# Twelve early column tiles instead of seven in the prologue of an adaLN and RWKV-7 kernel

## The chip, the cores and the metric

The kernel runs on one core of a Trainium2 chip. The metric is the device time of one execution in microseconds; the time of before is the median of three executions. A separate, profiled execution gives the trace: every instruction's start and end on TensorE (PE, its weight loads PEld), VectorE (DVE), ScalarE (ACT), GpSimd (POOL) and the queue SyncE (SP), which issues the DMA transfers. "L82" is line 82 of the kernel before.

## What is computed

One layer of a hybrid sequence model, for 128 context tokens and 256 latent tokens (T = 384 columns in all), with D = 2048 and 32 heads of 64. Cut to what matters:

```
mod = silu(c) @ ada_w + ada_b            # shift, scale, gate; for c and c_ctx
h   = rmsnorm(x, g) * (1 + scale) + shift
z   = h @ w_in                           # all projections, one wide matrix
r, k, v, wd, ad = token_shift(z[:N_SHIFTED])
g_a, b_gate, c_gate, x_b, g_b, m_a, m_b = split(z[N_SHIFTED:])
decay, a = f(tanh(wd) @ w2), sigmoid(a0 + ad @ a2)      # low rank, two directions
y   = bidirectional RWKV-7 scan(S0, r, decay, k, v, kk, a), group-normed, plus bonus
y_a = (y * silu(g_a)) @ w_out_a
y_b = (b_gate * conv3(c_gate * x_b) * silu(g_b)) @ w_out_b
out = x + gate * ((sigmoid(m_a) * y_a + sigmoid(m_b) * y_b) @ w_o)
```

The results are the normed outputs of both token groups and the scan's final context states.

## The kernel before

Everything is held transposed: 128 channels on the partitions, 384 tokens along the row. All large weights are float32 and are split into a high part (a cast by ACT) and a low part (a subtraction by DVE; `split`, L85). One product of a 128x128 weight block with 384 tokens is then three matmuls (`mm3`, L80): high by high, high by low, low by high. Such a triple is called a unit below, and 16 units, one for each block of 128 rows of D, make one column tile.

**Prologue (L370 to L389).** The modulation needs all of `ada_w`, and h only comes piece by piece: in round g of eight, PE multiplies four pieces of `ada_w` (tiles `raw_adah`, 128x4x512, PSUM tile `pada`), `make_h` turns row blocks 2g and 2g+1 of x into h (`h_hi`, `h_lo`), and from then on units on those two row blocks may run. Seven column tiles of `w_in` (three with the low-rank wd and ad, r of head-pair block 0, k of 0, v of 0 and 1) are accumulated meanwhile, each in a PSUM bank of its own over all eight rounds (`pe`). `early_load` fetches their rows for a round as one tile `eraw` and splits it; `pops(n)` takes n units from a list between the steps. All these loads stand in one queue on SP, in program order.

**Stream (`Stream`, L111).** The other column tiles come in pairs, 32 units a pair, through the tiles `raw`, `whi`, `wlo`: `rk{b}` (r and k of block b), `gv{b}` (the gate of block b and v of block b+1), and fillings for the convolution branch and the merge gates (`bc`, `bx`, `bg`, `gb`, `ma`, `mb`). `ds_.go(n)` issues the next n units; `ds_.until(tag)` goes on until a pair is done.

**Blocks (L937 on).** For each of 16 head-pair blocks b: `prep_b` builds the operands `pr` and `bk` of the chunk products, matmul `pA` starts the block, `prep_c` and a chain of small DVE operations (`U`, `ut`) with DMA in between invert the chunk matrices, then `scan` runs: matmul `pH` with its copies into `x`, `po`, `pbn`, `pX` with its copies into `A`, `pq`, and the rest. `scan` yields 3, 3 and 4 stream units after pH, po and pX (H0, H0, H1). Between the inversion and the scan stand a loop that streams until `gv{b}` is done, then `prep_a(b + 1)` (low-rank products `pl`, decay, the key norm `pn`, `kn`, and the scan `L`), then what is left of a window of 80 units. `norm` and, one block later, `finish` close a block.

**What sets the order.** PE executes the order in which the program is written (`manual_schedule`). The rows of DVE, ACT, POOL and SP are put in order by a scheduler, which places an instruction by the time at which it thinks it can start and by priority; on the chip each engine then runs its own list in that order. Buffers come from pools with a number of slots for each tag, and a new tile waits until the last user of its slot is done.

Of the kernel before, what the change touches and what calls it, by code (L numbers as in the profile page):

```python
# [56 lines left out]
def hybrid_step(ctx, tc, cst, x_prompt, x_sample, state_f, state_b, c, c_ctx, ada_w, ada_b, norm_g,  # L57
# [36 lines left out]
    PRO, WINDOW, FIRST, LAST = 32, 80, 24, 16  # L94
# [115 lines left out]
    ecols = ((O_WD, 3 * P), (O_R, P), (O_K, P), (O_V, 2 * P))  # L210
    NE = 7
    EW = NE * P
    banks = []
    for i in range(NE):
        pe = (pd if i < 3 else pps).tile([P, 512], F32, tag="d" if i < 3 else f"e{i}", name=f"pe_{i}")
        banks.append(pe)
    epss = [pe[:, 0:T] for pe in banks]

    xt = []
    for i, tg in enumerate(("ehi1", "elo1", "elo0")):  # L220
        xi = pp.tile([P, D], F32, tag=tg, name=f"xt{i}")
# [49 lines left out]
    def ada_load(rp, nm, cols, i, rbufs):  # L271
        raw = rp.tile([P, 4, 512], F32, tag="araw", name=f"raw_ada{nm}_{i}", bufs=rbufs)
# [870 lines left out]
```

## Time and profile before

| | before |
|---|---|
| median of 3 executions | 2264.56 us (2261.35 to 2266.23) |
| profiled execution | 2259.46 us, of which the span 2257.7 us |
| mean granted clock of PE | 0.996 |
| DVE, ACT, POOL busy | 1522.4, 1048.9, 118.6 us |
| DMA | 339.97 MB, mean 151 GB/s |

The span is the time from the first to the last instruction that the trace holds; the execution's own time is a little longer. A row of a timeline reads: start, duration, engine, line, operation, output <- inputs, shapes, number of equal instructions in a row, and in brackets the engine's idle time before it with what ended it. In a view of groups the mean duration in ns stands behind the sum.

### The profile page before, as it was taken

The page shows a single profiled execution, that of the slowest core. Times are in us where ns is not written, and L with a number is a line of the kernel's source. Part 1 is how long each engine was busy: PE and PEld are TensorE (multiplying, and loading weights), DVE is VectorE, ACT ScalarE, POOL GpSimd, SP SyncE. Part 2 cuts the span into 40 slices and gives each one's busy share as a digit, 9 for nine tenths or more (in the row PEclk, how much of TensorE's full clock was granted, in tenths as well). Part 3 has the DMA queues.
Part 4 walks back from the last instruction along what each step waited for, and adds up shares of the span by engine and source line. Part 5 has one row for each costly group of instructions (what it writes and reads, how often), then busy time and mean ns, then how long its engine had stood idle before and what let it go on. Part 6 is the DMA issues. An engine that isn't in the chain of part 4 may idle for free.

```text
span 2257.7 us, 40435 instructions
## 1 busy us (share of the span) xinstructions
PE 2187.7 (97%) x16084; PEld 2072.2 (92%) x16084; DVE 1522.4 (67%) x3096; ACT 1048.9 (46%) x1852; POOL 118.6 (5%) x115
## 2 busy tenths in 40 slices
PE   5999999999999999999999999999999999999998
PEld 3588999999999999999999999999999899889988
DVE  3249567777777778776878687777767774444444
ACT  4246445454545455454545454545455543333233
POOL 2001010101010100000010101010100000000000
PEclk9999999999999999999999999999999999999999
DMA  9963544444444444353444444444445465985633
GB/s 334 347 203 116 147 137 126 114 121 114 110 132 112 125 116 126 105 132 102 122 108 132 111 112 127 113 115 141 121 118 143 133 187 161 309 299 190 219 131 113
DMA packets 429646, 339.97 MB, mean 151 GB/s; under 512 B 84801, under 2 KB 411025, under 8 KB 428561
## 3 DMA queue, kind: packets, MB, share of 16 engines
q1 hardware_dynamic: 427968, 335.62, 50.6%
q8 instruction: 127, 2.08, 0.4%
q10 hardware_dynamic: 432, 1.57, 0.2%
q14 instruction: 63, 0.51, 0.1%
q0 software_dynamic: 1056, 0.19, 0.1%
HBM read 307.37 MB, written 29.36 MB: 149 GB/s over the span
## 4 chain that ended last, share of the span: by engine, by line
PE 90%; DMA 5%; DVE 2%; issue 2%; SPq 1%; ACT 1%; POOLq 0%; POOL 0%; DVEq 0%; ACTq 0%
PE d_rk L81 4%; PE d_gv L81 4%; PE d_gv L83 4%; PE d_gv L82 4%; PE d_rk L83 4%; PE d_rk L82 4%; DMA raw_adah<-in_ada_w_dram 3%; PE d_oa L81 2%; PE d_bx L81 2%; PE d_bg L81 2%; PE d_bc L81 2%; PE d_mb L81 2%; PE pq L822 2%; PE d_bg L83 2%; PE d_bg L82 2%; PE d_bx L83 2%
## 5 line engine op out<-in xcount | busy, mean ns | idle before, releaser
L716 DVE TENSOR_TENSOR ut<-U 48x30 f32<-48x30 f32 (+14 forms) x480 | 154.6, 322 | 16.2 <-DMA U<-ui 4.2
L81 PE MATMUL d_rk<-h_hi,whi_rk 128*128 128x384 f32 x480 | 164.3, 342 | 0.6 <-ACT lst L549 0.6
L718 DVE TENSOR_TENSOR U<-U,ut 48x30 f32<-48x30 f32 (+14 forms) x480 | 154.3, 321 | 10.8
L81 PE MATMUL d_gv<-h_hi,whi_gv 128*128 128x384 f32 x480 | 161.1, 336 | 0.0
L83 PE MATMUL d_gv<-h_hi,wlo_gv 128*128 128x384 f32 x480 | 160.8, 335 | 0.0
L82 PE MATMUL d_gv<-h_lo,whi_gv 128*128 128x384 f32 x480 | 160.7, 335 | 0.0
L83 PE MATMUL d_rk<-h_hi,wlo_rk 128*128 128x384 f32 x480 | 160.5, 334 | 0.0
L82 PE MATMUL d_rk<-h_lo,whi_rk 128*128 128x384 f32 x480 | 160.5, 334 | 0.0
L88 ACT CAST whi_gv<-raw_gv 128x1024 fp32r<-128x1024 f32 (+1 forms) x64 | 64.0, 999 | 141.1 <-PE d_rk L82 93.9
L89 DVE TENSOR_TENSOR wlo_rk<-raw_rk,whi_rk 128x1024 fp32r<-128x1024 f32 x60 | 72.9, 1218 | 44.6 <-ACT whi_rk L88 35.5
L88 ACT CAST whi_rk<-raw_rk 128x1024 fp32r<-128x1024 f32 x60 | 63.0, 1053 | 78.7 <-PE d_bx L82 16.4
L910 POOL TENSOR_TENSOR rs<-var,nhalf 128x6 f32<-128x6 f32 x16 | 21.2, 1326 | 1370.2 <-DVE var L908 1370.2
L81 PE MATMUL d_bg<-h_hi,whi_bg 128*128 128x384 f32 x256 | 92.8, 363 | 0.0
L81 PE MATMUL d_gb<-h_hi,whi_gb 128*128 128x384 f32 x256 | 92.5, 361 | 0.0
L81 PE MATMUL d_bc<-h_hi,whi_bc 128*128 128x384 f32 x256 | 92.4, 361 | 0.0
L81 PE MATMUL d_bx<-h_hi,whi_bx 128*128 128x384 f32 x256 | 92.3, 361 | 0.0
L81 PE MATMUL d_ma<-h_hi,whi_ma 128*128 128x384 f32 x256 | 92.0, 359 | 0.0
L81 PEld LDWEIGHTS d_rk<-h_hi,whi_rk 128*128 128x128 f32 x480 | 90.1, 188 | 1.8 <-ACT lst L549 0.9
L81 PEld LDWEIGHTS d_gv<-h_hi,whi_gv 128*128 128x128 f32 x480 | 90.5, 189 | 0.2
L81 PE MATMUL d_mb<-h_hi,whi_mb 128*128 128x384 f32 x256 | 90.6, 354 | 0.0
L82 PEld LDWEIGHTS d_gv<-h_lo,whi_gv 128*128 128x128 f32 x480 | 90.4, 188 | 0.0
L83 PEld LDWEIGHTS d_gv<-h_hi,wlo_gv 128*128 128x128 f32 x480 | 90.4, 188 | 0.0
(320 smaller groups left out, 6649.5 us busy)
## 6 DMA issues: line engine op xcount, KB each, us to landing
raw_adah<-in_ada_w_dram SPq DMA_DIRECT2D x64, 512.0 KB, 8.7
raw_rk<-in_w_in_dram SPq DMA_DIRECT2D x60, 512.0 KB, 5.3
raw_gv<-in_w_in_dram SPq DMA_DIRECT2D x60, 512.0 KB, 5.0
raw_ma<-in_w_in_dram SPq DMA_DIRECT2D x16, 1024.0 KB, 5.5
raw_mb<-in_w_in_dram SPq DMA_DIRECT2D x16, 1024.0 KB, 5.4
raw_bc<-in_w_in_dram SPq DMA_DIRECT2D x16, 1024.0 KB, 5.6
raw_bx<-in_w_in_dram SPq DMA_DIRECT2D x16, 1024.0 KB, 5.5
raw_bg<-in_w_in_dram SPq DMA_DIRECT2D x16, 1024.0 KB, 5.4
```

The source lines that it names most:

```text
L81: TE.matmul(out, wh, xh, start=start, stop=False)
L82: TE.matmul(out, wh, xl, start=False, stop=False)
L83: TE.matmul(out, wl, xh, start=False, stop=stop)
L88: S.copy(hi[0:rows], src)
L89: V.tensor_tensor(lo[0:rows], src, hi[0:rows].bitcast(F32), ALU.subtract)
L716: V.tensor_tensor(tv, U[:, 0:s, s:s + 1].broadcast_to([48, s, w]), U[:, s:s + 1, s + 1:].broadcast_to([48, s, w]), ALU.mult)
L718: V.tensor_tensor(U[:, 0:s, s + 1:], U[:, 0:s, s + 1:], tv, ALU.add)
L822: TE.matmul(pq[:, d, :], A[:, 0, f, :], sav[:, f, :], start=True, stop=True)
L910: G.tensor_tensor(rs[:], var[:], nhalf[:], ALU.pow)
```

## The change

The prologue now computes twelve column tiles: the seven of before, and the gate of block 0, r and k of block 1, and the two tiles of `ma0`. Five of them (wd/ad and ma0) keep a PSUM bank over all rounds. The other seven are summed in SBUF (`eacc`): in each round the two row blocks of a tile go into one of two rotating banks `er` with six matmuls, and then ACT copies (round 0) or DVE adds (rounds 1 to 7, 49 times) the bank to the sum. The early columns of a round come as three pieces of 128x2x512 through a ring of three; the norm's scratch tile uses the same ring; the pieces of `ada_w` use three buffers of their own and the two of the stream's `raw`. The units taken between the steps go from 14 to 24 a round. `rk1`, the gate of block 0 and `ma0`, 80 units, leave the stream. r, k, v and the gate move to a pool that is opened ahead of the prologue. `prep_a(b + 1)` moves behind the filling of the window, which becomes 79 units (93 in block 0, where it was 104), less the 12 that prep_a streams itself; it waits for `rk{b+1}` instead of `gv{b}`, and `finish(b - 1)` waits for `gv{b - 1}`.

```diff
-    PRO, WINDOW, FIRST, LAST = 32, 80, 24, 16
+    PRO, WINDOW, FIRST, LAST, PA = 32, 79, 14, 16, 12
...
-    ecols = ((O_WD, 3 * P), (O_R, P), (O_K, P), (O_V, 2 * P))
-    NE = 7
-    EW = NE * P
-    banks = []
-    for i in range(NE):
-        pe = (pd if i < 3 else pps).tile([P, 512], F32, tag="d" if i < 3 else f"e{i}", name=f"pe_{i}")
-        banks.append(pe)
-    epss = [pe[:, 0:T] for pe in banks]
+    ecols = (((O_WD, 3 * P), (O_GA, P)), ((O_R, 2 * P), (O_K, 2 * P)), ((O_V, 2 * P), (O_MA, 2 * P)))
+    banks, eacc = {}, {}
+    for i in (0, 1, 2, 10, 11):
+        banks[i] = (pd if i < 3 else pps).tile([P, 512], F32, tag="d" if i < 3 else f"e{i}", name=f"pe_{i}")
+    for i, (nm, b) in enumerate((("ga", 0), ("r", 0), ("r", 1), ("k", 0), ("k", 1), ("v", 0), ("v", 1))):
+        eacc[3 + i] = kp.tile([P, T], F32, tag=nm, name=f"{nm}_{b}")
+    epss = {i: banks[i][:, 0:T] for i in banks}
...
-        junk = pp.tile([P, 512], F32, tag="junk", name=f"junk_{s}")
+        junk = pp.tile([P, 2, 512], F32, tag="eraw", name=f"junk_{s}", bufs=3)
...
     def early_load(g):
-        raw = wp.tile([P, 2, EW], F32, tag="raw", name=f"eraw_{g}", bufs=2)
-        o = 0
-        for c0, w in ecols:
-            nc.sync.dma_start(raw[:, :, o:o + w], win[:, 2 * g:2 * g + 2, c0:c0 + w])
-            o += w
-        return split(raw[:], [P, 2, EW], f"ehi{g % 2}", f"elo{g % 2}", pp, f"{g}")
-
-    def early_mm(k, hl, i):
-        sl = slice(i * P, (i + 1) * P)
-        mm3(epss[i], hl[0][:, k % 2, sl], hl[1][:, k % 2, sl], h_hi[k], h_lo[k], k == 0, k == KC - 1)
+        res = []
+        for j, piece in enumerate(ecols):
+            raw = pp.tile([P, 2, 512], F32, tag="eraw", name=f"eraw_{g}_{j}", bufs=3)
+            o = 0
+            for c0, w in piece:
+                nc.sync.dma_start(raw[:, :, o:o + w], win[:, 2 * g:2 * g + 2, c0:c0 + w])
+                o += w
+            if g % 2 == 0:
+                res.append(split(raw[:], [P, 2, 512], "whi", "wlo", wp, f"e{g}_{j}"))
+            else:
+                hl = pp.tile([P, 2, 2, 512], F32R, tag=f"eo{j}", name=f"ehl_{g}_{j}")
+                S.copy(hl[:, 0], raw[:])
+                V.tensor_tensor(hl[:, 1], raw[:], hl[:, 0].bitcast(F32), ALU.subtract)
+                res.append((hl[:, 0], hl[:, 1]))
+        return res
+
+    def early_mm(g, e, hl, i):
+
+        hi, lo = hl[i // 4]
+        sl = slice(i % 4 * P, (i % 4 + 1) * P)
+        k = 2 * g + e
+        if i in epss:
+            mm3(epss[i], hi[:, e, sl], lo[:, e, sl], h_hi[k], h_lo[k], k == 0, k == KC - 1)
+            return
+        if e == 0:
+            banks["er"] = pps.tile([P, 512], F32, tag="er", name=f"er_{g}_{i}", bufs=2)
+        ps = banks["er"][:, 0:T]
+        mm3(ps, hi[:, e, sl], lo[:, e, sl], h_hi[k], h_lo[k], e == 0, e == 1)
+        if e == 1:
+            if g == 0:
+                S.copy(eacc[i][:], ps)
+            else:
+                V.tensor_tensor(eacc[i][:], eacc[i][:], ps, ALU.add)
...
+    def araw_load(g, ac, j):
+        if (4 * g + j) % 5 < 2:
+            return ada_load(wp, f"h{g}", ac, j, 2, "raw")
+        return ada_load(pp, f"h{g}", ac, j, 3)
...
-            pops(2 if g == 1 else (3, 4, 3, 2)[j])
+            pops(3 if g == 1 else (5, 6, 5, 4)[j])
         make_h(g, m5, pa)
-        pops(2)
-        queue += [(2 * g + e, hl, i) for e in range(2) for i in range(NE)]
+        pops(4)
+        keep, pas = [0, 1, 2, 10, 11], list(range(3, 10))
+        queue += [(g, 0, hl, i) for i in keep]
+        for n, i in enumerate(pas):
+            queue += [(g, 0, hl, i), (g, 1, hl, i)] + [(g, 1, hl, i2) for i2 in keep[n:n + 1]]
...
-    ds_.fills = fills
-    add_rk(1)
-    ds_.add("gv0", win, (O_GA,), hx, lambda i, ps: take_gate(0, ps))
+    ds_.fills = fills[1:]
+    ds_.done.add("gv0")
...
+    for i in range(2):
+        take_m(ma_d, "ma")(0, i, epss[10 + i])
     ctx_pro.close()
...
         if prev is not None:
+            ds_.until(f"gv{b - 1}")
             finish(b - 1, prev)
...
         if b < NB - 1:
-            while f"gv{b}" not in ds_.done:
+            while b > 0 and f"rk{b + 1}" not in ds_.done:
                 ds_.go(1)
                 n += 1
-            n += drive(prep_a(b + 1, nxt))
         w = WINDOW + (FIRST if b == 0 else LAST if b == NB - 1 else 0)
+        if b < NB - 1:
+            w -= PA
         if n < w:
             ds_.go(w - n)
+        if b < NB - 1:
+            drive(prep_a(b + 1, nxt))
```

PE in the prologue before, behind the first piece of `ada_w` in round 6 (`pada` is the modulation, `pe` an early tile, numbered by bank; `ehi` and `elo` are the parts of the seven columns of round 4):

```order
L289 MATMUL pada_784<-raw_adah_0_787,condw_pro 32x512 x4
L81 MATMUL pe_98<-h_hi_78,ehi_4_615 128x384
L82 MATMUL pe_98<-h_lo_82,ehi_4_615 128x384
L83 MATMUL pe_98<-h_hi_78,elo_4_616 128x384
L81 MATMUL pe_99<-h_hi_78,ehi_4_615 128x384
L82 MATMUL pe_99<-h_lo_82,ehi_4_615 128x384
L83 MATMUL pe_99<-h_hi_78,elo_4_616 128x384
L81 MATMUL pe_100<-h_hi_78,ehi_4_615 128x384
L82 MATMUL pe_100<-h_lo_82,ehi_4_615 128x384
L83 MATMUL pe_100<-h_hi_78,elo_4_616 128x384
L289 MATMUL pada_784<-raw_adah_1_803,condw_pro 32x512 x4
```

After, at the same place, from the second unit behind that piece on (`er` is a rotating bank, `whi_e_1` and `whi_e_2` are the second and the third of the three pieces):

```order
L81 MATMUL er_7_1076<-h_hi_78,whi_e_1_799 128x384
L82 MATMUL er_7_1076<-h_lo_82,whi_e_1_799 128x384
L83 MATMUL er_7_1076<-h_hi_78,wlo_e_1_800 128x384
L81 MATMUL er_7_1076<-h_hi_78,whi_e_1_799 128x384
L82 MATMUL er_7_1076<-h_lo_82,whi_e_1_799 128x384
L83 MATMUL er_7_1076<-h_hi_78,wlo_e_1_800 128x384
L81 MATMUL pe_102<-h_hi_78,whi_e_2_806 128x384
L82 MATMUL pe_102<-h_lo_82,whi_e_2_806 128x384
L83 MATMUL pe_102<-h_hi_78,wlo_e_2_807 128x384
L81 MATMUL er_8_1087<-h_hi_78,whi_e_2_806 128x384
L82 MATMUL er_8_1087<-h_lo_82,whi_e_2_806 128x384
L83 MATMUL er_8_1087<-h_hi_78,wlo_e_2_807 128x384
```

Before, each unit goes to a bank of its own, three of them between two pieces of `ada_w`; after, two units in a row fill a rotating bank (six matmuls), a unit on a fixed bank (`pe_102`) follows, and five units stand between the pieces.

DVE beside the scan of block 7, while block 8 is prepared, before: from the first row on the key norm on (`kn`, `kd`, `sig`, `L`, `bk` belong to block 8; `x`, `sav`, `bon`, `A` to block 7):

```order
L636 TENSOR_SCALAR kn_10260<-pn_10257 128x384
L651 TENSOR_SCALAR kd_0_10270<-sig_2_10237,par,omka 128x384
L638 RECIPROCAL kn_10260<-kn_10260 128x128 x2
L849 COPY x_7_9794<-pH_10283 32x6x32
L638 RECIPROCAL kn_10260<-kn_10260 128x128
L849 COPY x_7_9794<-pH_10283 32x6x32
L639 SCALAR_TENSOR_TENSOR kn_10260<-kk_10165,kn_10260 128x384
L806 TENSOR_TENSOR sav_9805<-po_1_0_10321,sav_9805 64x2x128
L652 TENSOR_TENSOR kd_0_10270<-k_10027,kd_0_10270 128x384
L653 TENSOR_TENSOR sig_2_10237<-kn_10260,sig_2_10237 128x384
L646 SCALAR_TENSOR_TENSOR L_1_10274<-cs,sig_1_10213 128x384
L859 TENSOR_TENSOR bon_10352<-pbn_10349,v_9017 128x384
```

and right behind them:

```order
L89 TENSOR_TENSOR wlo_bg_0_0_10336<-raw_bg_0_10333,whi_bg_0_0_10335 128x1024
L863 COPY A_9632<-pX_10354 32x6x32
L651 TENSOR_SCALAR kd_1_10278<-sig_3_10249,par,omka 128x384
L667 TENSOR_TENSOR bk_0_10712<-sig_2_10237,sig_0_10201 128x6x64
L863 COPY A_9632<-pX_10354 32x6x32
```

After, from the same first row on:

```order
L680 TENSOR_SCALAR kn_10566<-pn_10563 128x384
L695 TENSOR_SCALAR kd_0_10576<-sig_2_10543,par,omka 128x384
L682 RECIPROCAL kn_10566<-kn_10566 128x128 x3
L696 TENSOR_TENSOR kd_0_10576<-k_10296,kd_0_10576 128x384
L683 SCALAR_TENSOR_TENSOR kn_10566<-kk_10473,kn_10566 128x384
L690 SCALAR_TENSOR_TENSOR L_1_10580<-cs,sig_1_10509 128x384
L697 TENSOR_TENSOR sig_2_10543<-kn_10566,sig_2_10543 128x384
L712 TENSOR_TENSOR bk_0_11004<-kd_0_10576,sig_0_10497 128x6x64
L711 TENSOR_TENSOR bk_0_11004<-sig_2_10543,sig_0_10497 128x6x64
L695 TENSOR_SCALAR kd_1_10584<-sig_3_10555,par,omka 128x384
L89 TENSOR_TENSOR lwl_0_11618<-lraw_0_11615,lwh_0_11617 96x256
L696 TENSOR_TENSOR kd_1_10584<-k_10296,kd_1_10584 128x384
```

and right behind them:

```order
L697 TENSOR_TENSOR sig_3_10555<-kn_10566,sig_3_10555 128x384
L712 TENSOR_TENSOR bk_1_11010<-kd_1_10584,sig_1_10509 128x6x64
L711 TENSOR_TENSOR bk_1_11010<-sig_3_10555,sig_1_10509 128x6x64
L819 TENSOR_TENSOR kd_0_10576<-kd_0_10576,kd_1_10584 128x384
L820 SCALAR_TENSOR_TENSOR kd_0_10576<-kd_0_10576,par,r_10276 128x384
L893 COPY x_7_10113<-pH_10589 32x6x32 x2
L850 TENSOR_TENSOR sav_10124<-po_1_0_10627,sav_10124 64x2x128
L89 TENSOR_TENSOR wlo_gb_0_1_10533<-raw_gb_0_10526,whi_gb_0_1_10532 128x1024
L903 TENSOR_TENSOR bon_10648<-pbn_10645,v_9274 128x384
L907 COPY A_9935<-pX_10650 32x6x32
```

Before, the copies into x (L849) stand among the reciprocals, and the first copy into A (L863) ahead of all of `bk`. After, the rows for `bn` (L697), `bk` (L711, L712) and the bonus sum (L819, L820) of block 8 stand ahead of the copies into x (L893) and into A (L907).

More of the change, by code (lines that the diff above doesn't have):

```diff
@@ L199, in hybrid_step @@
     cT = cp.tile([P, 32], F32, tag="cT", name="cT")
+    ctx_kp = ExitStack()
+    kp = ctx_kp.enter_context(tc.tile_pool(name="kp", bufs=2))
     ctx_pro = ExitStack()
@@ L207, in hybrid_step @@
     nc.sync.dma_start(crow[16:32], c[0].rearrange("(k p) -> k p", p=P))
-    ecols = ((O_WD, 3 * P), (O_R, P), (O_K, P), (O_V, 2 * P))
-    NE = 7
-    EW = NE * P
-    banks = []
-    for i in range(NE):
-        pe = (pd if i < 3 else pps).tile([P, 512], F32, tag="d" if i < 3 else f"e{i}", name=f"pe_{i}")
-        banks.append(pe)
-    epss = [pe[:, 0:T] for pe in banks]
+    ecols = (((O_WD, 3 * P), (O_GA, P)), ((O_R, 2 * P), (O_K, 2 * P)), ((O_V, 2 * P), (O_MA, 2 * P)))
[5 more added lines that the diff above has]
+    epss = {i: banks[i][:, 0:T] for i in banks}
     xt = []
-    for i, tg in enumerate(("ehi1", "elo1", "elo0")):
-        xi = pp.tile([P, D], F32, tag=tg, name=f"xt{i}")
+    for i in range(3):
+        xi = pp.tile([P, D], F32, tag=f"eo{i}", name=f"xt{i}")
         nc.sync.dma_start(xi[:], x_prompt[0] if i == 0 else x_sample[0, (i - 1) * P:i * P])
@@ L269, in cond_weights, with ada_load @@
         return cw
-    def ada_load(rp, nm, cols, i, rbufs):
-        raw = rp.tile([P, 4, 512], F32, tag="araw", name=f"raw_ada{nm}_{i}", bufs=rbufs)
+    def ada_load(rp, nm, cols, i, rbufs, tag="araw"):
+        raw = rp.tile([P, 4, 512], F32, tag=tag, name=f"raw_ada{nm}_{i}", bufs=rbufs)
         o = 0
@@ L316, in x_norm @@
     def x_norm(s):
-        junk = pp.tile([P, 512], F32, tag="junk", name=f"junk_{s}")
+        junk = pp.tile([P, 2, 512], F32, tag="eraw", name=f"junk_{s}", bufs=3)
         for q in range(4):
-            S.activation(junk[:], xt[s][:, 512 * q:512 * q + 512], AF.Square, accum_out=ss4[:, s, q:q + 1])
+            S.activation(junk[:, q % 2, :], xt[s][:, 512 * q:512 * q + 512], AF.Square, accum_out=ss4[:, s, q:q + 1])
         V.tensor_reduce(ssx[:, s:s + 1], ss4[:, s:s + 1, :], AX.X, ALU.add)
@@ L328, in x_turn @@
         for q in range(4):
+            px = banks[10 + q] if q < 2 else pps.tile([P, 512], F32, tag="er", name=f"px_{s}_{q}", bufs=2)
             for i in range(4):
-                TE.transpose(banks[3 + q][:, i * P:(i + 1) * P], xt[s][:, (4 * q + i) * P:(4 * q + i + 1) * P], ident)
+                TE.transpose(px[:, i * P:(i + 1) * P], xt[s][:, (4 * q + i) * P:(4 * q + i + 1) * P], ident)
             (V.tensor_copy if q % 2 else S.copy)(xT[:, 4 * q:4 * q + 4, s * P:(s + 1) * P],
-                                                 banks[3 + q][:].rearrange("p (k t) -> p k t", t=P))
+                                                 px[:].rearrange("p (k t) -> p k t", t=P))
@@ L373, in hybrid_step @@
         ac = [(256 * g, 256), (D + 256 * g, 256)]
-        steps = ada_rows(condw, m5, ac, pa, lambda i: ada_load(pp, f"h{g}", ac, i, 5))
+        steps = ada_rows(condw, m5, ac, pa, lambda j: araw_load(g, ac, j))
         for j in range(4):
@@ L420, in shift, with take_shifted @@
                                    ALU.mult, ALU.add)
-    def take_shifted(nm, mi, store, b, ps):
-        t = box["sp"].tile([P, T], F32, tag=nm, name=f"{nm}_{b}", bufs=2)
+    def take_shifted(nm, mi, store, b, ps, t=None):
+        if t is None:
+            t = kp.tile([P, T], F32, tag=nm, name=f"{nm}_{b}")
         shift(t, ps, mi + b, MUP + mi + b, MUN + mi + b)
@@ L432, in take_gate @@
     def take_gate(b, ps):
-        t = box["sp"].tile([P, T], F32, tag="ga", name=f"ga_{b}", bufs=2)
+        if b == 0:
+            t = tmp("sg_0")
+            S.activation(t[:], ps, AF.Sigmoid)
+            V.tensor_tensor(ps, t[:], ps, ALU.mult)
+            ga_[b] = eacc[3]
+            return
+        t = kp.tile([P, T], F32, tag="ga", name=f"ga_{b}")
         S.activation(t[:], ps, AF.Sigmoid)
@@ L550, in hybrid_step @@
         stage.append(t)
-    for i, args in enumerate((("r", 0, r_, 0), ("k", 16, k_, 0), ("v", 32, v_, 0), ("v", 32, v_, 1))):
-        take_shifted(*args, epss[3 + i])
+    for i, args in ((4, ("r", 0, r_, 0)), (6, ("k", 16, k_, 0)), (8, ("v", 32, v_, 0)), (9, ("v", 32, v_, 1)),
+                    (5, ("r", 0, r_, 1)), (7, ("k", 16, k_, 1))):
+        take_shifted(*args, eacc[i][:], eacc[i])
+    take_gate(0, eacc[3][:])
     for m in range(4):
@@ L610, in prep_a @@
         bs = slice(b * P, (b + 1) * P)
-        r, k, v = r_[b], k_[b], v_[b]
+        k = k_[b]
         kk = sp.tile([P, T], F32, tag="kk", name=f"kk_{b}")
@@ L964, in hybrid_step @@
     ctx_sc.close()
+    ctx_kp.close()
     og = ctx.enter_context(tc.tile_pool(name="og", bufs=1))
```

## The prediction

> **What bounds the kernel now.** I read the page's busy line first, then TensorE's waits.
>
> ```profile
> PE 2187.7 (97%) x16084; PEld 2072.2 (92%) x16084; DVE 1522.4 (67%) x3096; ACT 1048.9 (46%) x1852; POOL 118.6 (5%) x115
> ```
>
> PE is busy for 97% of the span: time is won only where PE waits, where its clock is low, or where it gets fewer matmuls. The program order shows as many PE rows after as before, so the third way is closed. Waits of PE, longest sums first:
>
> ```profile
> engine line waited for: us in total, times, longest us
> PE pada L289 <- DMA raw_adah<-in_ada_w_dram: 23.4, 14, 10.4
> PE pq L822 <- issue: 16.6, 10, 2.0
> ```
>
> The first group lies in the prologue, which the change means to fill. The second lies in the chunk scan, one wait in ten of the sixteen blocks; "issue" means that no semaphore seen by the profile ended it. The windows show the prologue (columns: stretch and length, then busy PE, PEld, DVE, ACT, POOL, then PE's granted clock, DMA share, GB/s), and the timeline shows PE in it:
>
> ```profile
> 42.00:44.00 2.00, 1.61 (x8) 0.19 (x8) 1.04 (x1) 0.00 (x0) 0.00 (x0) 0.64 1.09 348
> 44.00:47.00 3.00, 3.00 (x18) 1.94 (x14) 0.00 (x0) 0.00 (x0) 0.00 (x0) 0.67 1.09 348
> ```
>
> ```profile
> 42.39 1.82 PE L289 MATMUL pada<-raw_adah,condw_pro 128*32 128x512 f32 x8 [3.94 <-DMA raw_adah<-in_ada_w_dram]
> ...
> 64.34 1.07 PE L289 MATMUL pada<-raw_adah,condw_pro 128*32 128x512 f32 x8
> 65.34 0.45 PE L81 MATMUL pe<-h_hi,ehi 128*128 128x384 f32 x1
> ...
> 65.99 0.34 PE L81 MATMUL pe<-h_hi,ehi 128*128 128x384 f32 x1
> ...
> 66.52 0.33 PE L81 MATMUL pe<-h_hi,ehi 128*128 128x384 f32 x1
> ...
> 91.70 0.28 PE L349 MATMUL pada<-cs,m 99*128 99x2 f32 x2
> ...
> 92.52 0.42 PE L81 MATMUL pe<-h_hi,ehi 128*128 128x384 f32 x1
> ...
> 148.14 0.45 PE L81 MATMUL d_rk<-h_hi,whi_rk 128*128 128x384 f32 x1 [0.61 <-ACT lst L549]
> ```
>
> DMA runs flat out at 348 GB/s. A round of the eight loads four ada pieces of 1.049 MB (128x4x512 floats) and 0.917 MB of early columns (128x2x896), 5.11 MB in all: 14.7 us. A unit (three matmuls on one 128x128 block) takes 66.52 - 65.99 = 0.53 us, and I use 0.525; an ada step takes 1.0 us (64.34 to 65.34), and starting the next unit adds about 0.21 around it (65.34 to 65.99 is 0.65, not 0.53, and the unit ahead is 0.09 longer). make_h takes 0.82 (91.70 to 92.52) and as much of a restart, 0.18. So PE's own round is 4 x 1.0 + 4 x 0.21 + 1.0 + 14 x 0.525 = 13.2 us: DMA sets the pace, by 1.5 us.
>
> **Prologue.** After, a round has 24 units: 4.0 + 0.84 + 1.0 + 12.6 = 18.4 us of PE, against 4 x 1.049 + 1.573 = 5.77 MB, 16.6 us of DMA. PE sets the pace.
>
> ```profile
> L289 PE MATMUL pada<-raw_adah,condw_pro 128*32 128x512 f32 x200 | 26.6, 603 | 8.6 <-DMA raw_adah<-in_ada_w_dram 8.4
> ```
>
> I anchor at the wait that ends at 42.39; behind it, from 45 to 147, PE waits 8.4 us more for DMA (last column: idle time and what ended it). Two rounds of early columns are queued ahead of the anchor's piece, 0.655 MB more each: 1.31 MB at 348 GB/s is 3.8 us, so the anchor moves to 46.2. The row-norm squares, which now share the early ring and so stand behind casts, hide in this wait of 3.9 us; uncovered, they cost what exceeds it. From the anchor PE has 1.6 us of low clock (the 5 us at 0.64 to 0.67), 2 ada steps and one make_h (2.8), six rounds of 4 x 1.0 + 0.82 (28.9), 186 units x 0.525 = 97.7, and 32 restarts x 0.214 = 6.9: 46.2 + 137.9 = 184.0. The same sum for before, with 108 units and the 8.4 us of waits, gives 42.4 + 1.6 + 2.8 + 28.9 + 56.7 + 6.9 + 8.4 = 147.7; the trace has 148.14 - 0.61 = 147.5. The early part ends 36.3 us later, and the stream behind it has 80 units fewer, 80 x 0.525 = 42.0. **Gain 5.7 us.**
>
> Seven tiles now go through two rotating banks, emptied by ACT (round 0) or DVE (49 adds):
>
> ```profile
> L89 DVE TENSOR_TENSOR elo<-eraw,ehi 128x1792 fp32r<-128x1792 f32 x8 | 16.2, 2026 | 32.0 <-ACT ehi L88 31.8 <-DMA raw_adah<-in_ada_w_dram 0.2
> L361 DVE TENSOR_TENSOR h_lo<-xT,h_hi 128x384 fp32r<-128x384 f32 x16 | 8.2, 555 | 7.2 <-ACT h_hi L360 7.2
> ```
>
> An add of 128x384 should cost what the 128x384 subtract (h_lo) did, 0.55 us, and a bank is wanted again three to four units (1.6 to 2.1 us) after its sixth matmul. Both groups take 24 us in eight rounds, so DVE is mostly free there, with 7 x 0.55 more a round. I take 0. At the far end each of the 49 adds stands behind a whole split of 2.0 us, 2.0 + 0.55 - 2.1 = 0.45 late, 22 us; a split stands near one add in three at most, which makes 7.
>
> **From the prologue to the first block.**
>
> ```profile
> 171.77 0.44 PE L81 MATMUL pl<-l_hi,lwh 96*128 96x384 f32 x1 [1.42 <-ACT lwh L88]
> ...
> 174.30 0.44 PE L83 MATMUL pl<-l_hi,lwl 96*128 96x384 f32 x1 [1.91 <-DVE lwl L89]
> ```
>
> ```profile
> 188.06 1.16 PE L695 MATMUL pA<-pr,bk 64*128 64x128 f32 x16 [1.49 <-DVE bk L667]
> ```
>
> ```profile
> 148.00:188.00 40.00, 35.10 (x188) 34.15 (x188) 32.65 (x73) 28.41 (x54) 1.96 (x7) 0.96 0.40 117
> ```
>
> ```profile
> 170.27 0.73 DVE L417 SCALAR_TENSOR_TENSOR r<-zs,par,r 128x127 f32<-128x127 f32 x2
> ```
>
> In this stretch DVE is nearly as long as PE, 32.7 of 40 us. Its work stays about equal: one multiply for the gate, no lo-parts of the single-tile stream. But the shifts of r1 and k1, which came from the stream at 170 us, right ahead of the chain to bk, now find their inputs in SBUF from the start. PE waited 1.42 + 1.91 + 1.49 = 4.8 us here, and a mean clock of 0.96 cost some 1.6. I take a little under half, **a gain of 2.8 us**; the ends are 0 (the chain over the low-rank weights, which the change leaves alone, is what is late) and 6.4.
>
> **The blocks.** Three blocks' starts (4, 5, 6), and the wait of one block (6) beside a block without (4):
>
> ```profile
> 632.04 1.16 PE L695 MATMUL pA<-pr,bk 64*128 64x128 f32 x16
> ```
>
> ```profile
> 736.58 0.60 PE L695 MATMUL pA<-pr,bk 64*128 64x128 f32 x6
> ```
>
> ```profile
> 843.20 1.05 PE L695 MATMUL pA<-pr,bk 64*128 64x128 f32 x14
> ```
>
> ```profile
> 689.82 0.34 PE L633 MATMUL pn<-sqh,bones_r 128*128 128x384 f32 x1
> ...
> 697.70 0.60 PE L822 MATMUL pq<-sav,A 128*128 128x128 f32 x4
> ```
>
> ```profile
> 900.99 0.34 PE L633 MATMUL pn<-sqh,bones_r 128*128 128x384 f32 x1
> ...
> 911.24 0.68 PE L822 MATMUL pq<-sav,A 128*128 128x128 f32 x4 [1.98 <-issue]
> ```
>
> The block without a wait takes 736.58 - 632.04 = 104.5 us, the next, 843.20 - 736.58, 106.6: a stalled block loses some 2.1 us. From pn to pq there are ten units and the same small matmuls, 7.88 us in block 4 and 10.25 in block 6, 2.4 more. What pq waits for stands on DVE: the copies that put pX into A.
>
> ```profile
> 690.37 0.56 DVE L636 TENSOR_SCALAR kn<-pn 128x384 f32<-128x384 f32 x1 [0.53 <-PE pn L634]
> ...
> 696.87 0.35 DVE L863 COPY A<-pX 32x192 f32<-32x192 f32 x1
> ```
>
> ```profile
> 901.54 0.56 DVE L636 TENSOR_SCALAR kn<-pn 128x384 f32<-128x384 f32 x1 [0.53 <-PE pn L634]
> 902.01 0.47 DVE L651 TENSOR_SCALAR kd<-sig,par,omka 128x384 f32<-128x384 f32 x1
> 902.40 2.57 DVE L638 RECIPROCAL kn<-kn 128x128 f32<-128x128 f32 x3
> ...
> 907.76 0.94 DVE L646 TENSOR_TENSOR_SCAN L<-cs,sig 128x384 f32<-128x384 f32 x1
> 908.63 0.53 DVE L667 TENSOR_TENSOR bk<-sig,sig 128x384 f32<-128x384 f32 x1
> 909.08 1.21 DVE L89 TENSOR_TENSOR wlo_gb<-raw_gb,whi_gb 128x1024 fp32r<-128x1024 f32 x1
> 910.21 0.55 DVE L859 TENSOR_TENSOR bon<-pbn,v 128x384 f32<-128x384 f32 x1
> 910.79 0.35 DVE L863 COPY A<-pX 32x192 f32<-32x192 f32 x1
> ```
>
> In block 6 DVE never rests from kn at 901.54 to the copy at 910.79 (9.25 us), and pq starts 0.1 us after the copy ends; in block 4 the same way takes 6.50 us, and pq is not delayed. So the loss of a block is the DVE work that stands in program order between kn and the first copy into A, less about 7.0 us.
>
> That work I add up from the program order, by the distance from one start to the next in this stretch: kn 0.48, a two-scalar op 0.39, a reciprocal 0.86, a scan 0.87, a split of 128x1024 1.13, bon 0.58, other 128x384 ops 0.47; for sav 0.36, a small copy 0.38 and a low-rank split 0.34, which are nearly the lengths of the rows. Before, the blocks give 6.1, 8.6 or 9.0. The sums leave small gaps out, so the threshold in this count is 6.55, and the excess over it of the fourteen scans 1 to 14 adds to 21.7 us, which fits 16.6 us of waits and the restarts behind them.
>
> After, block 8's preparation beside block 7's scan, whose rows the section on the change shows, has kn, two two-scalar ops (0.8), three reciprocals (2.6), a scan, eleven other 128x384 ops (5.2), a low-rank split, two x copies, sav, a split and bon: 13.0 us, against 8.6 before. More of the next block's prep_a and prep_b stands ahead of both the x copies and the A copies, while PE issues pn as close to pH as before. Scans 0 to 14 give 7.2, 10.4, 9.4, 10.6, 12.0, 12.7, 6.3, 13.0, 7.2, 8.6, 9.4, 10.4, 9.4, 9.4, 6.3; the excess over 6.55 adds to 44.5 us. PE's cover is unchanged, 3 + 3 + 4 units. **Loss 44.5 - 21.7 = 22.8 us.** Ends: 0, if the x copies' place costs nothing that the copies before them didn't, and 30, if the two-unit shorter window (158 instead of 160 units a block) also makes pH late in some.
>
> A long wait costs more than itself: after 3.94 us the clock was 0.64 and 0.67 (windows above), 1.6 us lost; after 1.98 us it was not:
>
> ```profile
> 911.00:914.00 3.00, 2.76 (x19) 2.79 (x20) 2.97 (x8) 1.98 (x5) 0.00 (x0) 1.00 0.00 0
> ```
>
> Three blocks lose 5.4 us or more, most of it in one wait, at pX: 3 x 1.6 = **4.7 us**, ends 0 and 10 (the six blocks that lose over 3.8). [...]
>
> What else moves: finish of a block now waits for the previous gate pair, which the stream reaches at the same place within two units; prep_a no longer waits for it, worth nothing, since PE showed no wait there. The two sigmoid tiles of ma0 go out in the prologue. At the end (oa, w_o) nothing changes, 0 within 3.
>
> **Sum:** -5.7 - 2.8 + 22.8 + 4.7 = +19.0 us. The durations are of the profiled run (2259.46 us, of which the span is 2257.7), 5.1 us under the median; on the median, 2264.6 + 19.0 = **2283.6 us**.
>
> **Rivals.**
> - *The order on DVE doesn't reach PE*: the extra work runs in DVE's idle time (67% busy), pX and pq come no later than before, and only -8.5 is left: 2256 us. It decides where the way from kn to the copy stays under 9 us. For it: DVE is not the bound. Against it: block 6, where that way was full and PE waited to the tenth of a microsecond. 0.12.
> - *Half of it*: the x copies run late, but the wait at pX lets DVE get ahead, so that the A copies are there at once and later waits of the block (the U loop) shrink. The loss of blocks is about 8 instead of 27.5: 2264. Against it: PE shows no other waits in the steady blocks from which it could be paid back. 0.12.
> - *The rotating banks stall PE in the prologue*: each pair waits for an add behind a split, a third of the far end and the clock with it, and +7 to +15 come on top: 2291 to 2298 us. It decides when an add lands over 2 us after its sixth matmul. 0.10.
> - The forecast has 0.66.
>
> The forecast's own range is 2272 to 2295. To hold 8 in 10 with the half case, it runs from 2259 to 2297. About 0.2% (4.5 us) is what a measurement of this kernel can tell from no change: faster by more 0.12, the same 0.13, slower 0.75.
>
> **What would show it.** Prologue: the last early matmul near 184, no DMA waits of pada after about 50, rows of er without waits. Blocks: waits at pX and pq (or "issue" there) of 2 to 6 us in blocks 1, 3, 4, 5 and 7, none in 6 and 14, and block lengths that spread from 103.5 to 110 us; granted clock under 0.9 after the longest. First pA at 184.0 + 37.9 = 222. If block lengths stay within 104 to 107 us, the reading of DVE's order is wrong; if the early part ends past 190, the sum for the banks is.

## The result, and the profile after

| | before | after |
|---|---|---|
| median | 2264.6 us (2261.35 to 2266.23) | 2283.68 us (2283.23 to 2284.46), 4 runs |
| ratio to before | | 1.0084 (95% interval 1.0071 to 1.0097) |
| profiled execution, span | 2259.46, 2257.7 | 2283.23, 2281.3 |
| mean granted clock | 0.996 | 0.990 |

The change costs 19.1 us on the medians. The two profiled executions are 23.6 us apart in their spans, because that of before lies 5.1 us under its median and that of after only 0.5. Of all the executions timed here one was far off, 4348.71 us of the last experiment (e8, some 2242 us otherwise), and the ratio of e8 leaves it out. PE's waits in the profile of after, the longest sums:

```profile
engine line waited for: us in total, times, longest us
PE pada L291 <- DMA raw_adah<-in_ada_w_dram: 13.0, 4, 9.6
PE pX L887 <- DVE x L893: 10.9, 12, 2.4
PE pH L887 <- DMA x<-uo: 9.8, 12, 2.1
PE pe L263 <- DVE crow L261: 7.1, 1, 7.1
PE pq L866 <- issue: 6.4, 7, 2.2
...
PE pX L887 <- ACT x L893: 2.6, 4, 1.1
...
PE er L81 <- DVE k L370: 1.1, 1, 1.1
```

Before, pq took 16.6 us of waits, pX 1.1 and pH 0.4. Now the waits in the scan are spread over pX (13.4 us in all), pH (9.8) and pq (7.4). The rotating banks `er` cost one wait of 1.1 us, and `pada` waits for its loads 10 us less than before.

The stages are read from the first row of each, in the timeline of PE after:

```profile
45.60 0.64 PE L291 MATMUL pada<-raw_adah,condw_pro 128*32 128x512 f32 x4 [0.51 <-DMA raw_adah<-in_ada_w_dram]
```

```profile
182.82 0.44 PE L81 MATMUL d_mb<-h_hi,whi_mb 128*128 128x384 f32 x1 [0.61 <-ACT lst L591]
```

```profile
221.83 0.38 PE L739 MATMUL pA<-pr,bk 64*128 64x128 f32 x2 [0.58 <-DVE bk L711]
```

The early part ends at 182.82 - 0.61 = 182.2 (before 147.5), 34.7 us later, and 42.0 us of stream are gone: a gain of 7.3. From there to the first pA it is 39.6 us (before 40.5): a gain of 0.9. Of the 80 units that left the stream, 53 are missing between the first and the sixteenth pA, where PE now has 2384 stream units for 2437, and 27 behind it. From the first to the sixteenth pA it is 1623.0 us (before 1611.5), with 53 units or 27.8 us less to do: a loss of 39.3. The rest takes 436.4 us (before 458.1), with 27 units or 14.2 us less to do: a gain of 7.5, of which 5.3 are waits that PE has there before and no longer has after. -7.3 - 0.9 + 39.3 - 7.5 = +23.6, the whole difference of the spans.

By kind, most of the loss in the blocks is of two sorts. The waits of PE there add up to 36.2 us, before to 19.9: 16.3 more, of which 9.4 at pH and 3.2 at pX and pq together. And the clock was low in eight stretches, before in one: in windows of 2 us, the length times what the granted clock lacks to 1 adds up to 15.4 us against 1.7, 13.7 more. This leaves 9.3 us that neither a named wait nor the low clock covers.

By place, it reads more simply. From pn to pq, scans 1 to 14 take 156.8 us on PE, before 131.0: 25.7 more. On DVE the way from kn to the end of the first copy into A takes 144.2 us in these scans, before 120.4: 23.8 more. In six of the fourteen, pq starts 0.1 us behind the end of that copy, as it does in the waiting blocks of before. Blocks 5 and 7 are among the six, though pH had waited 2.6 and 3.1 us in them. In block 5, DVE and PE:

```profile
841.03 0.35 DVE L907 COPY A<-pX 32x192 f32<-32x192 f32 x1
```

```profile
841.48 0.68 PE L866 MATMUL pq<-sav,A 128*128 128x128 f32 x4 [0.48 <-issue]
```

DVE has no named wait from kn (828.09) to this copy there, and its rows run in the order of the program (in the trace of after those beside the scan of block 7, from 1044.83 to 1058.65, stand row for row as listed for the change), so an earlier pH would not have let pq start earlier: the wait at pH lies beside the work on DVE and is no second cost. The other 13.6 us of the loss lie outside this stretch: 6.2 between pA and pn, 4.5 between pq and the next pA, and 2.9 in block 0.

Block 2 shows a wait and a low clock. PE, timeline:

```profile
500.07 0.34 PE L677 MATMUL pn<-sqh,bones_r 128*128 128x384 f32 x1
...
505.21 0.73 PE L887 MATMUL pX<-A,x 32*32 32x32 f32 x6
507.92 0.57 PE L887 MATMUL pX<-A,x 32*32 32x32 f32 x42 [1.98 <-DVE x L893]
511.76 0.63 PE L866 MATMUL pq<-sav,A 128*128 128x128 f32 x2
```

DVE beside it:

```profile
500.62 0.56 DVE L680 TENSOR_SCALAR kn<-pn 128x384 f32<-128x384 f32 x1 [0.52 <-PE pn L678]
...
505.33 0.56 DVE L697 TENSOR_TENSOR sig<-kn,sig 128x384 f32<-128x384 f32 x1
505.81 1.22 DVE L89 TENSOR_TENSOR wlo_bc<-raw_bc,whi_bc 128x1024 fp32r<-128x1024 f32 x1
507.06 0.42 DVE L850 TENSOR_TENSOR sav<-po,sav 64x256 f32<-64x256 f32 x1
507.51 0.36 DVE L893 COPY x<-pH 32x192 f32<-32x192 f32 x1
...
510.31 0.35 DVE L907 COPY A<-pX 32x192 f32<-32x192 f32 x1
```

And the windows, here and behind two other waits (PE's granted clock is the third number from the right):

```profile
292.00:298.00 6.00, 5.61 (x64) 5.46 (x65) 5.87 (x12) 1.82 (x7) 0.00 (x0) 0.72 0.52 144
507.00:513.00 6.00, 5.08 (x61) 5.04 (x62) 5.79 (x15) 4.45 (x11) 0.00 (x0) 0.72 0.00 0
829.00:836.00 7.00, 5.38 (x63) 5.21 (x64) 7.00 (x12) 2.79 (x7) 0.00 (x0) 0.58 0.63 171
```

The way from kn to the first copy into A takes 9.69 us (the sum from the order was 9.4). The second copy into x stands behind a split and sav, so pX waits 1.98 us. Behind it the granted clock is 0.50 for 3.4 us (509.21 to 512.62), which is a mean of 0.72 over 6 us; from pn to pq it is 11.69 us instead of 7.88. pq no longer waits, since the slow units ahead of it, with some 0.32 us from one matmul to the next for 0.18 before, take up the time.

### The profile page after: what moved, and what is told of

It reads as the page before. It is cut to its first block, busy times and chain, and to the rows that moved or that the text cites. A ratio compares the mean times of both kernels' runs of the same rounds, so it can differ in the third digit from the quotient of the medians.

```text
span 2281.3 us, 40535 instructions
## 1 busy us (share of the span) xinstructions
PE 2206.8 (97%) x16084; PEld 2086.5 (91%) x16084; DVE 1548.5 (68%) x3149; ACT 1051.4 (46%) x1865; POOL 119.1 (5%) x115
## 4 chain that ended last, share of the span: by engine, by line
PE 81%; DVE 11%; DMA 3%; issue 2%; ACT 1%; SPq 1%; POOL 0%; POOLq 0%; DVEq 0%; ACTq 0%
PE d_rk L81 3%; PE d_rk L83 2%; PE d_rk L82 2%; PE d_gv L81 2%; PE d_gv L83 2%; PE d_gv L82 2%; PE d_oa L81 2%; PE pA L739 2%; PE pq L866 2%; PE d_oa L83 2%; PE d_oa L82 2%; PE d_gb L81 2%; PE d_mb L81 2%; PE d_bc L81 2%; PE d_gb L83 2%
## 5 line engine op out<-in xcount | busy, mean ns | idle before, releaser
L762 DVE TENSOR_TENSOR U<-U,ut 48x30 f32<-48x30 f32 (+14 forms) x480 | 154.6, 322 | 11.4
L83 PE MATMUL d_gv<-h_hi,wlo_gv 128*128 128x384 f32 x464 | 155.8, 336 | 0.0
L82 PE MATMUL d_gv<-h_lo,whi_gv 128*128 128x384 f32 x464 | 155.7, 335 | 0.0
L81 PE MATMUL d_rk<-h_hi,whi_rk 128*128 128x384 f32 x448 | 155.6, 347 | 0.0
L83 PE MATMUL d_rk<-h_hi,wlo_rk 128*128 128x384 f32 x448 | 149.9, 335 | 0.0
L82 PE MATMUL d_rk<-h_lo,whi_rk 128*128 128x384 f32 x448 | 149.9, 335 | 0.0
L81 PE MATMUL d_ob<-ybh,whi_ob 128*128 128x384 f32 x256 | 88.8, 347 | 0.0
L81 PE MATMUL d_oa<-yah,whi_oa 128*128 128x384 f32 x256 | 87.5, 342 | 0.0
```

The costliest lines, as they stand in the source:

```text
L81: TE.matmul(out, wh, xh, start=start, stop=False)
L82: TE.matmul(out, wh, xl, start=False, stop=False)
L83: TE.matmul(out, wl, xh, start=False, stop=stop)
L762: V.tensor_tensor(U[:, 0:s, s + 1:], U[:, 0:s, s + 1:], tv, ALU.add)
```

## The experiments

All are timed against the kernel before on the same chip. The "excess" is what the prediction used: DVE's work in program order from kn to the first copy into A, less 6.55 us, summed over the scans.

**e1: the move alone, on the prologue of before.**

```diff
-    PRO, WINDOW, FIRST, LAST = 32, 80, 24, 16
+    PRO, WINDOW, FIRST, LAST, PA = 32, 79, 24, 16, 12
...
+            ds_.until(f"gv{b - 1}")
             finish(b - 1, prev)
...
-            while f"gv{b}" not in ds_.done:
+            while b > 0 and f"rk{b + 1}" not in ds_.done:
...
-            n += drive(prep_a(b + 1, nxt))
...
+        if b < NB - 1:
+            w -= PA
...
+        if b < NB - 1:
+            drive(prep_a(b + 1, nxt))
```

> The prologue of before (seven early tiles, all streams kept), and of the change only the move of prep_a behind the window's filling with WINDOW 79 and PA 12, the wait for gv{b-1} ahead of finish and none for gv{b}. Theory (the place and length of the window set the order on DVE, and that order costs the time): the DVE work between kn and the first copy into A, counted in the program order as in the prediction, has an excess of 41.2 us over the fifteen scans against 21.7 before, so +19.5 us, and +8 for the low clock behind the waits: about 2292 us (2282 to 2298). Rival (the new prologue with its streams taken out and its shifted phases makes the blocks long): 2264.6 within 5 us.

2293.08 us, ratio 1.0121 (1.0104 to 1.0138), as the theory had it. The loss in the blocks is that of the change, without a new prologue: from the first to the sixteenth pA it takes 16.8 us longer than before with 43 units or 22.6 us less to do, a loss of 39.4. The first pA stands at 188.3, as before, so nothing is gained ahead of it. The blocks have waits at pH (12.3 us) and pX, and seven stretches of low clock.

**e2: the prologue alone.** The changed kernel with the lines of e1 taken back, WINDOW 80, FIRST 24.

> The twelve early tiles of the change, but prep_a, its wait for gv{b}, WINDOW 80 and FIRST 24 as before. Theory: the prologue keeps its gain of some 7 us, the steady blocks 3 to 13 wait as before (2.1 to 2.4 us in most); the order shows 6 us more excess in blocks 1 to 4 and 17.1 us instead of 8.6 in scan 14, which may or may not become a wait: 2258 to 2270 us. Rival (the new prologue itself costs the time of the blocks): 2280 us or more.

2278.54 us, ratio 1.0058 (1.0043 to 1.0073): outside what the theory gave, and near the rival's number. But the rival is wrong about the place. Blocks 3 to 13 take 104.6 to 108.6 us and wait at pq as before. Block 14 takes 119.4 for 106.6 us, in one wait that the kernel before doesn't have, followed by a clock of 0.53 over 10 us:

```profile
PE d_ob L81 <- ACT ybh L544: 10.3, 1, 10.3
```

`ob` is the first product with w_out_b, on the result `yb` that goes through DRAM; with 80 units gone from the stream it comes while block 14 still runs. In SP's queue the loads of yb first stand behind a load of w_out_b that waits 8.4 us for its buffer, and then wait 5.7 us themselves, until a product on DVE is done. Of the waits of the queue from 1770 to 1800 us, these loads (L543) have

```profile
SPq L543 <- DVE bk L711: 7.1, 2, 5.7
```

e3 shows the first of the two alone.

**e3: two units a block more.** The changed kernel with

```diff
-    PRO, WINDOW, FIRST, LAST, PA = 32, 79, 14, 16, 12
+    PRO, WINDOW, FIRST, LAST, PA = 32, 81, 14, 16, 12
```

> The changed kernel with WINDOW 81 for 79 and nothing else: 160 instead of 158 stream units a block, as before the change. In the program order the excess of DVE work between kn and the first copy into A falls from 44.6 to 2.3 us. Theory (DVE's order and the two units of cover missing at pH are the loss): the waits at pH, pX and pq and the low clock behind them go, those of before too: 2264.6 - 7 (prologue) - 19 (waits of before) - 2 (clock of before) = 2236 us (2232 to 2245). Rival (the move of prep_a costs by itself, or the waits come from the U chain's DMAs and not from the order): 2272 to 2284 us.

2255.45 us, ratio 0.9955 (0.994 to 0.9969). Between the two. Blocks 1 to 13 are as the theory had them: 105.1 to 106.5 us, no wait above 1.2, no low clock. Block 14 takes 117.2 us. The DMA issues of SP there:

```profile
1757.47 17.34 SPq L101 DMA_DIRECT2D raw_ob<-in_w_out_b_dram  x3
1774.91 0.52 SPq L543 DMA_DIRECT2D yst_b<-yb_d  x1
```

Three loads of w_out_b stand in the queue ahead of the loads of yb (`yst_b`). The second and the third wait 6.5 and 9.4 us for their buffers, and hold what stands behind them. In the changed kernel the order is the other way round, and it has no such wait.

**e4: DVE's order made worse.** PE's order stays row for row, and POOL's too. DVE's list differs at 383 of its 3149 places, ACT's at 194 of 1868, and SP's issues at 21 of 898.

```diff
-            drive(prep_a(b + 1, nxt))
+            drive(prep_a(b + 1, nxt), 300)
```

> The changed kernel with a priority of 300 in the scheduler for prep_a(b + 1): PE's order and all units of cover are the same as in the changed kernel, row for row; on DVE still more of prep_a and prep_b stands ahead of the copies into x and A (excess 71.5 instead of 44.6 us). Theory (the order on DVE decides): 16 us (what of the 27 doesn't lie beside a wait at pH) to 27 us of waits more, and 5 to 10 us of low clock: 2304 to 2320 us. Rival (the waits come from the shorter cover of the U chain alone): 2283.7 within 5 us.

2328.12 us, ratio 1.0281 (1.0264 to 1.0299): 44 us over the changed kernel, more than the theory's 20 to 36. pX waits 4.9 us in blocks 0, 1 and 8, and the clock is low in 13 of 15 blocks. ACT makes half of the copies into x, but of 51.0 us of waits at pX the view puts 44.2 down to those of DVE:

```profile
PE pX L887 <- DVE x L893: 44.2, 28, 3.9
```

The fifteen stretches from pn to pq are 47.9 us longer than in the changed kernel, of 50.0 us between the two spans. The excess of 27 us more was about right: the way on DVE grew by 25.5. The clock was again put too low: 25.6 us more are lost by it, for 5 to 10.

**e5 and e6: the same window, four units apart.** Both are e3 with another FIRST; from block 1 on PE does the same, shifted by four units against the pairs of the stream.

```diff
-    PRO, WINDOW, FIRST, LAST, PA = 32, 79, 14, 16, 12
+    PRO, WINDOW, FIRST, LAST, PA = 32, 81, -2, 16, 12   # e5
+    PRO, WINDOW, FIRST, LAST, PA = 32, 81, -6, 16, 12   # e6
```

> WINDOW 81 as in e3, and FIRST -2 for 14: block 0 streams 16 units less, so that w_out_b comes 16 units later. In the program order all excess is 0 (every scan has 6.2 to 6.3 us of DVE work between kn and the first copy into A), and on SP the loads yst_b stand behind one load of w_out_b, where e3 has three. Theory (e3's block 14 was long, 117.2 for 105.4 us, because the loads of yb stood in SP's queue behind a load of w_out_b that waited for its buffer): 2255.5 - 11.8 = 2243 us (2238 to 2248), no wait of d_ob above 3 us. Rival (ybh waits for the last use of h, whose place it takes): a wait of d_ob of 8 us stays, 2252 to 2256 us.

> As e5, but FIRST -6: 4 units fewer in block 0, and every later block has the same 160 units and the same cover, only shifted by 4 units against the stream's pairs. In the program order 13 of 15 scans have 8.6 us of DVE work between kn and the first copy into A. Theory (DVE's order alone makes the waits): 14 waits of 2.05 us at pq and a low clock behind some of them: e5 + 28 to 36 us. Rival (cover of the U chain, or the moved prep_a by itself, makes them): e5 within 4 us.

e5: 2240.0 us, ratio 0.9901 (0.9884 to 0.9919), the best kernel of this study: 24.7 us under before, where the change was 19.1 over it. Block 14 takes 107.5 us and no d_ob wait is left. The queue now reads:

```profile
1758.63 0.39 SPq L101 DMA_DIRECT2D raw_ob<-in_w_out_b_dram  x1
1761.27 0.34 SPq L530 DMA_DIRECT2D mb_d<-mb  x1
1761.73 4.65 SPq L543 DMA_DIRECT2D yst_b<-yb_d  x4
```

e6: 2263.0 us, ratio 0.9997 (0.9987 to 1.0006), 23 us over e5; the forecast of 28 to 36 was somewhat high, because the waits at pq were 1.1 us for 2.05 and none lowered the clock in blocks 1 to 13 (1.00 from 817 to 823, around that of block 5). Its blocks take 106.6 to 108.0 us for 105.3 to 106.0. DVE in block 5 of e5:

```profile
805.19 0.56 DVE L680 TENSOR_SCALAR kn<-pn 128x384 f32<-128x384 f32 x1 [1.05 <-PE pn L678]
...
809.97 0.36 DVE L893 COPY x<-pH 32x192 f32<-32x192 f32 x1
810.37 0.56 DVE L903 TENSOR_TENSOR bon<-pbn,v 128x384 f32<-128x384 f32 x1
810.84 0.94 DVE L682 RECIPROCAL kn<-kn 128x128 f32<-128x128 f32 x1
811.81 0.35 DVE L907 COPY A<-pX 32x192 f32<-32x192 f32 x1
```

and of e6:

```profile
811.77 0.56 DVE L680 TENSOR_SCALAR kn<-pn 128x384 f32<-128x384 f32 x1 [3.26 <-PE pn L678]
...
818.12 0.94 DVE L690 TENSOR_TENSOR_SCAN L<-cs,sig 128x384 f32<-128x384 f32 x1
818.99 0.52 DVE L903 TENSOR_TENSOR bon<-pbn,v 128x384 f32<-128x384 f32 x1
819.43 0.54 DVE L696 TENSOR_TENSOR kd<-k,kd 128x384 f32<-128x384 f32 x1
819.90 0.54 DVE L697 TENSOR_TENSOR sig<-kn,sig 128x384 f32<-128x384 f32 x1
820.47 0.35 DVE L907 COPY A<-pX 32x192 f32<-32x192 f32 x1
```

6.62 us in e5, 8.70 in e6. In e6 the scheduler put a scan and several products of the next block ahead of the copy, which in e5 come behind it, and pq waits 1.10 us for it in nearly every block: in 13 of the scans 1 to 14 it starts 0.1 us behind the end of the copy. The shift of PE's order moves ACT's and SP's lists too, so the times of the pair alone would not single out DVE; this place does.

**e7 and e8: the cover of pH.** In both, units move from ahead of pH to behind pX, and a block keeps its 160.

```diff
-    PB0, PB1, H0, H1, CH0, CH1 = 14, 6, 3, 4, 2, 4
-    PRO, WINDOW, FIRST, LAST, PA = 32, 81, -2, 16, 12
+    PB0, PB1, H0, H1, CH0, CH1 = 14, 6, 3, 6, 2, 4      # e7; e8: 3, 5
+    PRO, WINDOW, FIRST, LAST, PA = 32, 79, -2, 16, 12   # e7; e8: 80
```

> e5 with two units moved within each block: WINDOW 79 for 81, and 6 for 4 units between pX and pq. A block keeps its 160 units; from pA to pH there are 85, as in the changed kernel, for 87 in e5. The excess of DVE work stays without effect (7.2 us against a cover of 7.6). Theory A (the waits at pH, 9.8 us in the changed kernel, come from the two units of cover that are missing): pH waits of 8 to 12 us in all and a low clock behind some, 2250 to 2262 us. Theory B (they come from what else stands in the queues of DVE and SP while the U chain runs, in blocks whose phase shifts): no wait at pH above 0.5 us in the steady blocks, e5 within 4 us.

> e5 with one unit moved: WINDOW 80 for 81, and 5 for 4 units between pX and pq; 86 units to pH. In the program order the copies into x stand 3.3 us behind kn instead of 4.8, so that the wait of 0.35 us at pX goes in 13 blocks: 4.5 us less than e5, 2235 us (2232 to 2240). Rival (theory A of e7): a wait at pH of 0.3 to 0.5 us a block takes its place, 2240 to 2247 us.

e7: 2256.01 us, ratio 0.9965 (0.9951 to 0.9979). There is not one wait at pH, with the 85 units (from the second group of pA's rows on) that the changed kernel has too. So the missing two units alone don't make pH late, and theory A falls. The time didn't follow theory B either: e7 is 16 us over e5, between its first and sixteenth pA, in blocks of 106.0 to 107.1 us; 10.5 of the 16 lie behind pq. The profile names some 7 of these: pX waits 0.2 longer in every block, and a wait at pu of about 0.7 comes in six blocks. The rest stays open.

e8: 2242.71 us, ratio 0.9903 (0.9886 to 0.9919). The wait at pX went, as forecast, but small ones at pq and po took its place, and the time is that of e5 within the spread.

Where pH does wait, the transfer into x was issued late. In block 5 of the changed kernel, 770.51 to 880.50, the last two issues for x on SP were

```profile
826.47 1.38 SPq L774 DMA_DIRECT2D x<-uo  x1
...
828.91 0.47 SPq L774 DMA_DIRECT2D x<-uo  x1
```

58.4 us after its pA, and in block 5 of e7 (pA at 753.91) 52.6 us:

```profile
806.51 0.47 SPq L774 DMA_DIRECT2D x<-uo  x1
```

From the traces, the chain on U ended 48.9 us after pA in the first and 46.0 in the second, with 14.9 and 11.4 us of other DVE work laid into it. So 2.9 of the 5.8 us between the two issues come from the chain, and the place of other work in DVE's list would account for them. Another 1.6 come from the store of U (`uo`) behind it: issued 0.5 us after a load of the stream it took 5.7 us to land, and 1.7 us after one in e7 4.1. Neither was tested by itself, and what makes pH late stays open.

## Why the prediction was right, and where it was lucky

The number was met to 0.1 us (2283.6 for 2283.68), closer than its steps deserve. The stages were off by -1.6, +1.9, +11.8 and -7.5 us, which makes +4.6, and the choice of the base took off those 4.6. That is luck. The mechanism of the main term is not.

- **Prologue**: a gain of 5.7 was forecast, 7.3 measured. The anchor came at 45.6 (46.2 forecast). The low clock behind it, which the sum kept (1.6 us), moved to 27.9 to 34.8 us (0.51 there), ahead of the anchor. The banks' term was right at almost 0 (1.1 us).
- **To the first block**: 2.8 forecast, 0.9 measured, within its ends. First pA was forecast at 222 (the terms, 184.0 + 40.5 - 2.8, give 221.7), and came at 221.83, because the errors of the two stages cancel.
- **Blocks**: 22.8 + 4.7 = 27.5 forecast, 39.3 measured. The sign, the cause (DVE's order) and the count held. The count has 22.8 us more DVE work between kn and the first copy into A; the way between them grew by 23.8 in scans 1 to 14, and scan by scan it is 0 to 0.8 us over its count (to the start of the copy 12.9 for 12.7 in block 5, 6.75 for 6.3 in block 6). e4, and e5 against e6, change that order with PE's work the same, or the same but for a shift of four units, and the time goes with it.
- **Where PE spends it** was wrong. The waits at pX and pq grew by 3.2 us, not by 22.8: PE spent the time of DVE's way in waits at pH too, and in rows at a granted clock of 0.50, which use up what would have been the next wait. So the 2 to 6 us at pX and pq that were to show in blocks 1, 3, 4, 5 and 7 came as 0.5 to 1.8. The low clock took 13.7 us instead of 4.7. That only waits of some 4 us cost more than themselves was an estimate from two waits, 3.94 us with a fall and 1.98 without; in the same profile the clock fell behind one of 1.97, in block 2 (0.50 from 486.29 to 489.71). The text had pH only at the far end, and for a reason (two units less of cover) that e7 doesn't bear out.
- **Outside the stretch from pn to pq** the blocks lost 13.6 us and the end gained 7.5, where the sum had 0 for both.
- **The base**: on the profiled runs the forecast was +19.0 and the measured difference 23.6. The medians differ by 19.1, since the profiled execution of before lies 5.1 us under its median. This made up for the missing 4.6 us.

The rivals: DVE's order does reach PE (e4), so the first falls. The half case had a point, that a wait at pX keeps pq from waiting, but PE lost the time of DVE's way all the same. The banks didn't stall. What no rival had was that the loss isn't bound to the move of prep_a: the same change with 160 units a block and another phase (e5) gains 1%.

## What to carry to other kernels

An engine that is 67% busy can still set the pace where its program order puts unrelated work ahead of a copy that the bound engine waits for in a short chain; add up that work between the two ends of the chain, and compare it with the cover. Measure the loss between the same two ends, too: the labels of the waits between them shift from one row to the next. If a scheduler writes that order, two units in a window or four units of phase can be worth more than 20 us here (the change against e3, e5 against e6), so a change ought to be tried at several phases before it is judged. Work taken out of a stream also brings forward what stands at its end, and the loads queued there (e2, e3).

## What the runs showed of the hardware

The clock fell behind waits as short as 0.9 us: in the profile of after pX waits 0.87 us up to 292.12, and the granted clock is 0.50 from 294.17 to 297.58.

Counted over the profiles of before, after and e1 to e6, from 260 to 1860 us, with waits of at least 0.3 us less than 7 us apart taken as one group, and "low" for a mean clock under 0.9 in the 6 us behind the group:

| longest wait of the group | at pq: low | at pH or pX: low |
|---|---|---|
| 0.8 to 1.3 us | 0 of 21 | 7 of 11 |
| 1.3 to 2.45 us | 4 of 24 | 12 of 16 |
| over 2.45 us | none seen | 6 of 6 |

The products pH and pX are rows of 32x32 matmuls, a sixteenth of a 128x128 one, and stand beside the wait there; pq is 128x128.

A count on the granted clock in the traces tells most of the cases apart. In each of the ten profiles all low stretches start at whole multiples of 3.413 us from one another, wherever the waits lie: in that of after those at 294.17, 399.99 and 509.21 are 31 and 32 times 3.413 us apart. Take, then, the 3.413 us up to each such instant, and weight the time of each matmul (from its start to that of the next, less idle time) by its rows times its columns in the trace, as a share of 128x128. Between the first and the sixteenth pA the clock fell 37 times, and 36 of the windows ahead of a fall have at most 0.44 by this count (the one of before 0.44, the eight of after 0.01 to 0.44; the one above it 0.53). Of 4635 windows at full clock without a fall behind them, two have less than 0.44. PE's time without the weights doesn't part them: windows ahead of a fall then go up to 0.73, and 53 without a fall lie under that. The one with 0.73 is in the profile of after, from 615.02 to 618.44: PE is busy for 2.49 of its 3.42 us, 48 of its 57 matmuls are 32x32, and the granted clock behind it is 0.50 up to 621.85. The weights were found on these same traces, and no kernel was made to test them; in the prologue, with its 128x32 matmuls, they part less well: in the profile of before three windows there have 0.37 to 0.41 (up to 35.73, 73.28 and 117.65) and no fall behind them.

Equal waits fare differently by where they lie. Of the three waits of 1.97 to 1.98 us at pq before, the first lies almost whole in one window, which leaves 1.49 us of PE (0.44), and the clock falls. The other two reach over the edge of a window, which leaves 1.72 and 1.56 us (0.50 and 0.46). The windows of PE (length, busy time, granted clock), the first with the one behind it:

```profile
482.88:486.29 3.41, 1.49 (x10) 1.00 0.00 0
486.29:489.71 3.42, 3.42 (x15) 0.50 0.00 0
909.55:912.96 3.41, 1.72 (x12) 1.00 0.00 0
1332.80:1336.21 3.41, 1.56 (x9) 1.00 0.00 0
```
